# Head norms on ScalarE, and the gates of two channel tiles ahead of the key projection, in a streaming encoder layer

## The chip, the cores and the metric

The kernel runs on one NeuronCore of a Trainium2 chip. The metric is device time in microseconds (us) for one execution; lower is better. Engines: TensorE (PE; its weight loads are PEld), VectorE (DVE), ScalarE (ACT), GpSimd (POOL) and SyncE (SP), whose queue issues the transfers.

## The reference

One layer of a chunk-causal encoder, for a prompt of 1024 tokens and a sample batch of 8 x 16 tokens (1152 tokens, nine tiles of 128). What matters here is the first sub-layer:

```python
h = rmsnorm(x, g_mix)
z = h @ w_in                                   # 1024 -> 2560
zq, zk, zv, zu = jnp.split(z, [512, 1024, 1536], axis=-1)
q = rmsnorm(zq.reshape(B, T, 4, 2, 64), g_q)   # each head map of 64 on its own
k = rmsnorm(zk.reshape(B, T, 4, 2, 64), g_k)   # k is an output too
...                                            # differential attention on q, k, v
a, gate = jnp.split(zu, 2, axis=-1)
c = a * jax.nn.sigmoid(gate)                   # 512 channels
c_hist = jnp.concatenate([c_past, c], axis=1)
cv = jax.nn.silu(layernorm(depthwise_causal_conv(c_hist, w_conv, b_conv), ln_g, ln_b))   # 31 taps
x = x + jnp.concatenate([o, cv], axis=-1) @ w_out
```

A memory cross-attention and a squared-ReLU MLP follow. All is in float32. `rmsnorm` divides by the root of the mean square plus 1e-6.

## The kernel before

**Products.** Every large product is made of three matmuls, on operands that are split in a high and a low part (`mm3`, lines 123 to 125). The split of a weight unit (`load_w`) is a transfer into one of four raw buffers, a cast on ScalarE (line 113) and a subtraction on VectorE or GpSimd (line 116); it lands in a pool of eight units ("w") or, for some, in a second of two ("wx"). In the stages looked at here the subtraction is on VectorE.

**Projections.** The normalised and transposed input stays in on-chip memory. After channel tiles 0 and 1 of the gates come three projections, `wi` = 0, 1, 2 for Q, K and V, each with eight weight units and nine token tiles. `project(wi, wu, t)` makes 24 matmuls into one PSUM bank (of eight in the pool). For Q and K it then takes the norm of each of the eight 64-wide heads: ScalarE squares the whole 512 (line 374), VectorE reduces to eight sums (376), GpSimd adds epsilon (377) and raises to the power -1/2 (`rpow`, line 139), VectorE multiplies the bank with the eight values into `zn` (380). `zn` is stored (383, 385), and for K VectorE also makes the output `ko` with the gain (388). The tiles `sq` and `ko` share a tag with two buffers. For V ScalarE copies the bank (366).

**Convolution.** The 512 channels are four channel tiles `ct` of 128. For each, `start_conv` reserves the gate output `cp` (prompt) and `cs` (samples), two buffers each, has GpSimd clear the first 30 columns (344), and loads four weight units. `history` brings the past. `gated` multiplies, for three groups of three token tiles, the gate half and then the linear half, each into a bank; ScalarE takes a tanh of the first (290, one buffer) and VectorE writes the product into `cp` and `cs` (293, 296). `conv_taps` then runs 31 taps on VectorE, each one instruction of 1024 columns for the prompt (305 for the first, 307) and one of 128 for the samples (326, 328), and stores the accumulators (331, 332). The prompt's accumulator `acc` has one buffer. `conv_state` writes the last gate outputs out.

**Order.** The taps are a chain of generators, `taps`; one step of it is two taps, and 16 steps are a channel tile. Tile 0's first 768 columns are done while the gates of tiles 0 and 1 run. After each token tile of a projection `TP[wi]` steps are taken, with TP = (4, 2, 2). Channel tile 2 has its gates between Q and K, tile 3 between K and V. This is the order in which the program is written; the order of each engine's queue is drawn up from it by a scheduler that estimates when an instruction is ready, and is then fixed.

**Attention.** After the V projection the pools of the projections and of the convolution are given back, and their memory is taken by the attention stage: the prompt's scores and softmax (`attend`), the products with the values by way of the transposed weights `wT` (`values`, lines 699 to 704), the sample batch's attention over the cache, and `conv_norm`, which reads the stored accumulators. Reuse of memory waits for its last reader, the accumulators' store among them.

Of the kernel before, what the change touches and what calls it, by code (L numbers as in the profile page):

```python
# [12 lines left out]
AF = mybir.ActivationFunctionType  # L13
ALU = mybir.AluOpType
# [4 lines left out]
P = 128  # L19
# [17 lines left out]

WB, RB, VB, KB, UB = 8, 4, 3, 4, 2

TP, HP = (4, 2, 2), 2  # L40

EL = 3

# [21 lines left out]
def kernel(  # L65
# [187 lines left out]
    def history(ct, cs):  # L253
        hist = cv.tile([120, 2, P], F32, name=f"hist{ct}", tag="hist", bufs=1)
        for j in range(2):
            sp.dma_start(hist[:, j, :], cache_conv[0, 4 * j:4 * j + 4, :, ct * P:(ct + 1) * P].rearrange("b t c -> (b t) c"))
        ps = bank(f"hi{ct}")
        for j in range(2):
            pe.transpose(ps[:, j * 120:(j + 1) * 120], hist[:, j, :], ident[:120, :120])
        dve.tensor_scalar_mul(cs[:, :, 0:30], ps[:, :240].rearrange("p (b t) -> p b t", t=30), 2.0)  # L260
# [56 lines left out]
    def conv_taps(ct, cp, cs, lo=0):  # L317
        if lo == 0:
            accs[ct] = cv.tile([P, 1024], F32, name=f"acc{ct}", tag="acc", bufs=1)
        acs = cv.tile([P, P], F32, name=f"acs{ct}", tag="acs")  # L320
        av = acs.rearrange("p (b t) -> p b t", t=16)
        for j in range(31):
            prompt_tap(ct, cp, j, lo, 1024)
            wj = wc[:, ct, j:j + 1]
            if j == 0:
                dve.tensor_scalar(av, cs[:, :, 0:16], wj, col("b_conv", ct), op0=ALU.mult, op1=ALU.add)
            else:
                dve.scalar_tensor_tensor(out=av, in0=cs[:, :, j:j + 16], scalar=wj, in1=av, op0=ALU.mult, op1=ALU.add)
            if j % 2:
                yield  # L330
        sp.dma_start(dacc[ct, :, 0:1024], accs[ct])
        sp.dma_start(dacc[ct, :, 1024:1152], acs)
        yield
# [7 lines left out]
    def start_conv(ct):  # L341
        cp = cv.tile([P, 1054], F32, name=f"cp{ct}", tag="cp")
        cs = cv.tile([P, 8, 46], F32, name=f"cs{ct}", tag="cs")
        pool.memset(cp[:, 0:30], 0.0)
        raws = load_wz(ct)
        if ct:
            convs[ct] = (cp, cs, split_wz(ct, raws))
        else:
            convs[ct] = (cp, cs, raws)

    def run(it):
        for _ in it:
            pass
# [6 lines left out]
    def project(wi, wu, t):  # L360
        ps = bank(f"z{wi}_{t}")
        for k in range(KT):
            mm3(ps, tok(hT, k, t, 0), tok(hT, k, t, 1), wu[k][:, 0, :], wu[k][:, 1, :], k == 0, k == KT - 1)
        zn = wk.tile([P, 512], F32, name=f"zn{wi}_{t}", tag="zn", bufs=3)
        if wi == 2:
            act.copy(zn, ps)
            sp.dma_start(vf[t].rearrange("t h e -> t (h e)"), zn)
            if t < 8:
                sp.dma_start(dv[t * P:(t + 1) * P, :], zn)
            else:  # L370
                pool.tensor_copy(v8, zn)
            return
        sq = wk.tile([P, 512], F32, name=f"sq{wi}_{t}", tag="sq")
        act.activation(sq, ps, AF.Square, scale=0.125)
        ms = sm(8, "ms8")
        dve.tensor_reduce(out=ms, in_=sq.rearrange("p (a d) -> p a d", a=8), axis=AX.X, op=ALU.add)
        pool.tensor_scalar_add(ms, ms, EPS)
        rs = sm(8, "rs8")
        rpow(rs, ms, 8)
        dve.tensor_mul(zn.rearrange("p (a d) -> p a d", a=8), ps.rearrange("p (a d) -> p a d", a=8),  # L380
                       rs.unsqueeze(2).broadcast_to([P, 8, 64]))
        if t < 8:
            sp.dma_start(dq[wi][t * P:(t + 1) * P, :], zn)
        else:
            sp.dma_start(d8[wi], zn)
        if wi == 1:
            ko = wk.tile([P, 512], F32, name=f"ko{t}", tag="sq")
            dve.tensor_mul(ko.rearrange("p (a d) -> p a d", a=8), zn.rearrange("p (a d) -> p a d", a=8),
                            gkb.unsqueeze(1).broadcast_to([P, 8, 64]))
            sp.dma_start(kf[t].rearrange("t h c -> t (h c)"), ko)  # L390
# [139 lines left out]
    for wi in range(3):  # L530
        wu = load_qkv(wi)
        for t in range(NT):
            project(wi, wu, t)
            if t == 0:
                for ct in ((0, 1), (2,), (3,))[wi]:
                    conv_state(ct, *convs[ct][:2])
            run(islice(taps, TP[wi]))
            if wi == 2 and t == EL:
                load_half(1, 0, 0)
                load_half(0, 0, 0)  # L540
                for j in range(KB):
                    load_keys(0, j)
        if wi < 2:
            ct = wi + 2
            start_conv(ct)
            history(ct, convs[ct][1])
            for g in range(3):
                run(gated(ct, g, *convs[ct]))
            taps = chain(taps, conv_taps(ct, *convs[ct][:2]))
    run(taps)  # L550
    p1.close()
    pg.close()
# [1111 lines left out]
```

## Time and profile before

| | |
|---|---|
| timed runs | 1578.28, 1606.75, 1607.65 us (median 1606.75) |
| the profiled execution | 1578.97 us, its span 1577.2 us, mean granted TensorE clock 0.985 |
| TensorE busy | 1501.8 us (95% of the span), weight loads 1296.0 (82%) |
| VectorE busy | 1086.6 us (69%), 2020 instructions |
| ScalarE busy | 731.9 us (46%), 1530 instructions |
| GpSimd busy | 242.9 us (15%), 374 instructions |
| transfers | 237.88 MB, 151 GB/s over the span |

In the profiled execution the Q projection runs from 80 to 132 us, the gates of channel tile 2 to 157, K to 207.5, the gates of tile 3 to 233.7, and V to 284.5. A busy TensorE is not one at its peak, as matmuls overlap; idle time of an engine counts only where the end waits for it. Times in rows are us from the start of the span unless marked ns; what stands in square brackets at the end of a timeline row is the engine's idle time ahead of it and what ended it.

### The profile page before, as it was taken

Reading aid. Unit: us, or ns where it says so; the run is one execution under the profiler, and the core shown is the slowest. Engines: PE = TensorE matmul, PEld = TensorE weight load, DVE = VectorE, ACT = ScalarE, POOL = GpSimd, SP = SyncE. Lnnn points to the kernel's source line nnn. Section 1 sums busy time; section 2 is a strip of 40 time slices with the busy share of each in tenths; the row PEclk is TensorE's granted clock in tenths of the full one; section 3 lists DMA queues with packets and bytes.
Section 4 is the critical chain, followed back from the end, with each engine's and each line's share of the span. In section 5 each row is a group of like instructions: output and inputs, shape, how many; then the busy total and the mean of one; then the engine's idle time right before and its main releaser. Section 6 shows DMA issues by size and latency. Waiting matters only on the chain.

```text
span 1577.2 us, 25642 instructions
## 1 busy us (share of the span) xinstructions
PE 1501.8 (95%) x9326; PEld 1296.0 (82%) x9326; DVE 1086.6 (69%) x2020; ACT 731.9 (46%) x1530; POOL 242.9 (15%) x374
## 2 busy tenths in 40 slices
PE   6999999779898899999999899999999999999998
PEld 6989898457686787787678899999999888778887
DVE  5899899967566664534857786676566556996565
ACT  5312021478677742634656444444353444544442
POOL 3051530041544431131011000000000000000000
PEclk9999999899999999999999999999999999999999
DMA  6333242477775733112432554444574566743343
GB/s 201 129 95 107 85 142 110 157 253 251 237 227 160 252 108 104 47 47 88 138 104 95 156 196 154 154 149 130 167 231 136 170 206 215 241 130 109 119 141 94
DMA packets 187121, 237.88 MB, mean 151 GB/s; under 512 B 23851, under 2 KB 101717, under 8 KB 186996
## 3 DMA queue, kind: packets, MB, share of 16 engines
q1 hardware_dynamic: 186996, 236.25, 46.9%
q8 instruction: 73, 1.20, 0.3%
q14 instruction: 52, 0.43, 0.1%
HBM read 172.59 MB, written 63.60 MB: 150 GB/s over the span
## 4 chain that ended last, share of the span: by engine, by line
PE 78%; DVE 7%; DMA 5%; ACT 4%; POOL 2%; issue 2%; SPq 1%; DVEq 0%; ACTq 0%
PE p L124 13%; PE p L125 13%; PE p L123 13%; PE pj L123 3%; PE pj L125 3%; PE pj L124 3%; PE z L123 2%; PE z L124 2%; PE z L125 2%; PE zu L125 2%; PE zu L123 2%; DVE acc L307 2%; PE zu L124 2%; PE po L704 2%; PE kT L768 1%
## 5 line engine op out<-in xcount | busy, mean ns | idle before, releaser
L124 PE MATMUL p<-Bp,Ap 128*128 128x512 f32 x448 | 175.8, 392 | 1.4 <-DVE Bp L1532 1.4
L125 PE MATMUL p<-Bp,Ap 128*128 128x512 f32 x448 | 174.9, 391 | 0.0
L307 DVE SCALAR_TENSOR_TENSOR acc<-cp,wc,acc 128x1024 f32<-128x1024 f32 (+2 forms) x150 | 158.7, 1066 | 0.7
L123 PE MATMUL p<-Bp,Ap 128*128 128x512 f32 x448 | 158.1, 390 | 1.0 <-ACT Bp L1531 1.0
L1531 ACT CAST Ap<-w_xb 128x512 fp32r<-128x512 f32 x112 | 69.5, 621 | 160.6 <-PE p L125 138.8
L1532 DVE TENSOR_TENSOR Ap<-w_xb,Ap 128x512 fp32r<-128x512 f32 x112 | 77.3, 690 | 90.0 <-ACT Ap L1531 90.0
L123 PE MATMUL p<-b_t,s 128*128 128x288 f32 x384 | 114.4, 298 | 4.5 <-DVE o L1378 4.5
L124 PE MATMUL p<-b_t,s 128*128 128x288 f32 x384 | 114.3, 298 | 0.0
L125 PE MATMUL p<-b_t,s 128*128 128x288 f32 x384 | 113.9, 298 | 0.3 <-DVE s L1285 0.3
L124 PEld LDWEIGHTS p<-Bp,Ap 128*128 128x128 f32 x448 | 84.6, 189 | 21.4 <-DVE Bp L1532 3.8
L123 PEld LDWEIGHTS p<-Bp,Ap 128*128 128x128 f32 x448 | 84.1, 188 | 18.8 <-ACT Bp L1531 1.4
L125 PEld LDWEIGHTS p<-Bp,Ap 128*128 128x128 f32 x448 | 84.6, 189 | 17.5
L123 PE MATMUL z<-wqkv,h 128*128 128x512 f32 x216 | 86.0, 398 | 0.0
L125 PE MATMUL z<-wqkv,h 128*128 128x512 f32 x216 | 85.4, 395 | 0.0
L124 PE MATMUL z<-wqkv,h 128*128 128x512 f32 x216 | 85.3, 395 | 0.0
L123 PEld LDWEIGHTS p<-b_t,s 128*128 128x128 f32 x384 | 72.9, 190 | 4.7 <-ACT s L1284 4.7
L123 PE MATMUL p<-b_b,a 128*128 128x288 f32 x256 | 75.7, 296 | 0.0
L124 PE MATMUL p<-b_b,a 128*128 128x288 f32 x256 | 75.7, 296 | 0.0
L125 PE MATMUL p<-b_b,a 128*128 128x288 f32 x256 | 75.6, 296 | 0.0
L1368 ACT ACTIVATE o<-o 128x576 f32<-128x576 f32 x64 | 43.8, 685 | 68.4 <-DVE o L1378 28.2
L124 PEld LDWEIGHTS p<-b_t,s 128*128 128x128 f32 x384 | 73.1, 190 | 0.0
L125 PEld LDWEIGHTS p<-b_t,s 128*128 128x128 f32 x384 | 72.3, 189 | 0.6 <-DVE s L1285 0.6
(511 smaller groups left out, 4237.8 us busy)
## 6 DMA issues: line engine op xcount, KB each, us to landing
kr<-in_cache_k_dram SPq DMA_DIRECT2D x32, 512.0 KB
vu<-in_cache_v_dram SPq DMA_DIRECT2D x32, 512.0 KB
w1t<-in_w_ff_dram SPq DMA_DIRECT2D x32, 512.0 KB
w_xb<-ds SPq DMA_DIRECT2D x64, 256.0 KB
da<-o SPq DMA_DIRECT2D x48, 256.0 KB
w_xb<-da SPq DMA_DIRECT2D x48, 256.0 KB
ds<-o SPq DMA_DIRECT2D x32, 256.0 KB
dxr<-XP SPq DMA_DIRECT2D x18, 256.0 KB
```

What stands on the lines that cost most here:

```text
L123: pe.matmul(out, lh, rh, start=first, stop=False)
L124: pe.matmul(out, lh, rl, start=False, stop=False)
L125: pe.matmul(out, ll, rh, start=False, stop=last)
L307: dve.scalar_tensor_tensor(out=out, in0=cp[:, lo + j:hi + j], scalar=wj, in1=out, op0=ALU.mult, op1=ALU.add)
L704: pe.matmul(po, wT[:, j * P:(j + 1) * P], vss[h][jb][:, j], start=4 * jb + j == 0, stop=4 * jb + j == i)
L768: pe.transpose(ps[:, h * 256 + t * P:h * 256 + (t + 1) * P], kr[:, t, (2 * hp + h) * P:(2 * hp + h + 1) * P], ident)
L1368: act.activation(c, c, AF.Relu)
L1531: act.copy(u[:, 0], src)
L1532: dve.tensor_sub(u[:, 1], src, f32(u[:, 0]))
```

## The change

The reduction and the product of the norm go from VectorE to ScalarE. In place of one Square over 512 columns there are eight over 64, each with its sum taken by the instruction (`accum_out`), and in place of the product on VectorE eight copies, each scaled by its head's value. GpSimd's two steps stay. The gates of channel tiles 2 and 3 both come between Q and K, with three tap steps after each of their six groups (GP = 3); TP becomes (3, 2, 2). The convolution state of tile 3 is written in the K projection instead of the V projection.

```diff
--- before.py
+++ after.py
@@ -37,7 +37,7 @@
 
 WB, RB, VB, KB, UB = 8, 4, 3, 4, 2
 
-TP, HP = (4, 2, 2), 2
+TP, HP, GP = (3, 2, 2), 2, 3
 
 EL = 3
 
@@ -371,14 +371,15 @@
                 pool.tensor_copy(v8, zn)
             return
         sq = wk.tile([P, 512], F32, name=f"sq{wi}_{t}", tag="sq")
-        act.activation(sq, ps, AF.Square, scale=0.125)
         ms = sm(8, "ms8")
-        dve.tensor_reduce(out=ms, in_=sq.rearrange("p (a d) -> p a d", a=8), axis=AX.X, op=ALU.add)
+        heads = [slice(a * 64, a * 64 + 64) for a in range(8)]
+        for a, c in enumerate(heads):
+            act.activation(sq[:, c], ps[:, c], AF.Square, scale=0.125, accum_out=ms[:, a:a + 1])
         pool.tensor_scalar_add(ms, ms, EPS)
         rs = sm(8, "rs8")
         rpow(rs, ms, 8)
-        dve.tensor_mul(zn.rearrange("p (a d) -> p a d", a=8), ps.rearrange("p (a d) -> p a d", a=8),
-                       rs.unsqueeze(2).broadcast_to([P, 8, 64]))
+        for a, c in enumerate(heads):
+            act.activation(zn[:, c], ps[:, c], AF.Copy, scale=rs[:, a:a + 1])
         if t < 8:
             sp.dma_start(dq[wi][t * P:(t + 1) * P, :], zn)
         else:
@@ -532,7 +533,7 @@
         for t in range(NT):
             project(wi, wu, t)
             if t == 0:
-                for ct in ((0, 1), (2,), (3,))[wi]:
+                for ct in ((0, 1), (2, 3), ())[wi]:
                     conv_state(ct, *convs[ct][:2])
             run(islice(taps, TP[wi]))
             if wi == 2 and t == EL:
@@ -540,13 +541,14 @@
                 load_half(0, 0, 0)
                 for j in range(KB):
                     load_keys(0, j)
-        if wi < 2:
-            ct = wi + 2
-            start_conv(ct)
-            history(ct, convs[ct][1])
-            for g in range(3):
-                run(gated(ct, g, *convs[ct]))
-            taps = chain(taps, conv_taps(ct, *convs[ct][:2]))
+        if wi == 0:
+            for ct in (2, 3):
+                start_conv(ct)
+                history(ct, convs[ct][1])
+                for g in range(3):
+                    run(gated(ct, g, *convs[ct]))
+                    run(islice(taps, GP))
+                taps = chain(taps, conv_taps(ct, *convs[ct][:2]))
     run(taps)
     p1.close()
     pg.close()
```

## Rows read from the trace of the kernel before

**Rows 1.** the chain of waits that ended last: each engine's share of the span

```profile
PE 78%; DVE 7%; DMA 5%; ACT 4%; POOL 2%; issue 2%; SPq 1%; DVEq 0%; ACTq 0%
```

**Rows 2.** stretch, length; busy PE, PEld, DVE, ACT, POOL; clock, DMA share, GB/s

```profile
157.00:207.50 50.50, 50.50 (x220) 40.54 (x219) 42.72 (x63) 7.42 (x14) 25.53 (x14) 1.00 0.25 84
...
233.70:284.50 50.80, 50.76 (x220) 40.43 (x218) 47.43 (x62) 5.24 (x10) 2.47 (x3) 1.00 0.31 112
285.00:300.00 15.00, 9.30 (x66) 6.39 (x66) 13.27 (x21) 9.36 (x20) 1.69 (x3) 0.89 0.78 246
300.00:312.00 12.00, 8.73 (x45) 5.19 (x42) 11.56 (x22) 4.15 (x10) 0.97 (x1) 0.59 0.28 100
312.00:333.00 21.00, 13.99 (x154) 8.84 (x153) 13.85 (x26) 11.58 (x28) 8.71 (x11) 0.91 0.57 186
333.00:345.00 12.00, 10.08 (x80) 6.73 (x79) 7.14 (x21) 11.37 (x27) 3.35 (x7) 1.00 1.07 340
...
365.00:400.00 35.00, 32.02 (x364) 26.19 (x364) 24.26 (x72) 27.16 (x71) 7.37 (x16) 1.00 0.86 268
```

**Rows 3.** VectorE's last taps: its groups after 284.5, timeline, and the chain at 327

```profile
L307 DVE SCALAR_TENSOR_TENSOR acc<-cp,wc,acc 128x1024 f32<-128x1024 f32 x22 | 28.1, 1280 | 0.1
...
325.84 1.28 DVE L307 SCALAR_TENSOR_TENSOR acc<-cp,wc,acc 128x1024 f32<-128x1024 f32 x1
...
332.26 0.29 DVE L701 COPY wT<-pT 128x128 f32<-128x128 f32 x1 [4.48 <-DMA dacc<-acc]
...
327.15 5.03 DMA dacc<-acc
```

**Rows 4.** VectorE's groups of 80 to 284.5 us: busy, mean ns, idle before

```profile
L380 DVE TENSOR_TENSOR zn<-z,rs 128x512 f32<-128x512 f32 x18 | 12.4, 687 | 9.0 <-POOL rs L139 8.9
L376 DVE TENSOR_REDUCE ms<-sq 128x8 f32<-128x512 f32 x18 | 12.2, 681 | 1.8 <-ACT sq L374 1.7
```

**Rows 5.** timeline of GpSimd and VectorE where a buffer is waited for

```profile
138.04 0.12 POOL L344 MEMSET cp<- 128x30 f32 x1 [1.41 <-DVE acc L307]
...
272.50 0.81 DVE L305 TENSOR_SCALAR acc<-cp,wc,cols 128x1024 f32<-128x1024 f32 x1 [3.05 <-DMA dacc<-acc]
```

**Rows 6.** ScalarE's timeline in the attention, and its Square in the projections (ns)

```profile
334.81 0.37 ACT L715 ACTIVATE o<-po,f 128x128 f32<-128x128 f32 x1 [0.34 <-POOL f L139]
335.08 1.25 ACT L800 ACTIVATE sp<-sp,smn 128x1152 f32<-128x1152 f32 x1
...
338.80 0.28 ACT L708 ACTIVATE o<-po 128x128 f32<-128x128 f32 x1
338.97 0.19 ACT L708 ACTIVATION_READ_ACCUMULATOR o<-po 128x1 f32 x1
339.06 0.61 ACT L113 CAST wmk<-wmk_1r 128x512 fp32r<-128x512 f32 x1
...
L374 ACT ACTIVATE sq<-z x18: 574/598/602, 86.5 to 220.6; 128x512 f32<-128x512 f32 x18
```

**Rows 7.** GpSimd's two steps of a norm, Q tile then K tile

```profile
95.42 0.26 POOL L377 TENSOR_SCALAR ms<-ms 128x8 f32<-128x8 f32 x1
95.76 1.67 POOL L139 TENSOR_TENSOR rs<-ms,neghalf 128x8 f32<-128x8 f32 x1
...
171.75 1.20 POOL L377 TENSOR_SCALAR ms<-ms 128x8 f32<-128x8 f32 x1 [3.47 <-DVE ms L376]
173.03 2.80 POOL L139 TENSOR_TENSOR rs<-ms,neghalf 128x8 f32<-128x8 f32 x1
```

**Rows 8.** ScalarE and TensorE at the junction of the K projection and the gates

```profile
212.85 0.62 ACT L113 CAST wqkv<-wqkv_2r 128x512 fp32r<-128x512 f32 x1 [6.71 <-DMA wqkv_2r<-in_w_in_dram]
...
212.75 0.45 PE L125 MATMUL zu<-h,wz 128*128 128x384 f32 x1 [0.63 <-DVE wz L116]
```

## The prediction, made before the changed kernel ran

> **What bounds the kernel now.** I read the chain of waits first. TensorE carries 78% of it, VectorE 7% [rows 1], so a step counts only where TensorE waits, and the next view is the table by stage [rows 2]. The K projection (157 to 207.5 us) is TensorE without a gap: 50.50 busy of 50.50 us, 50.5/9 = 5.61 us a token tile. The V projection (233.7 to 284.5) is the same, 50.76 of 50.80. So in the stages that the change edits there is nothing for TensorE to win. Just behind them there is: from 285 to 333 us it is busy 9.30 + 8.73 + 13.99 = 32.0 us of 48, while VectorE is full (13.27 of 15, 11.56 of 12) until 312. The granted clock is 0.89, 0.59 and 0.91 of full there: from 300 to 312 mostly the lower level of 1.2 GHz, after 15 us in which TensorE worked 9.30.
>
> What VectorE does there is convolution taps of the last channel tile. Between 284.5 and 340 us it still runs 22 of them, 28.1 us in all; the last starts at 325.84, the store of the accumulator lands 5.03 us after 327.15, and only then, at 332.26, does VectorE make the first transposed weight tile wT, having waited 4.48 us for that landing [rows 3]. The wT tiles take over the memory of the convolution pool, so no product with the values runs before. The late taps cost twice: they share VectorE with the scores of the first attention tiles, and they lock the second half of attention.
>
> **What is removed.** Per tile of Q and K, VectorE loses the reduction and the product with the inverse norm: 18 x (0.681 + 0.687) = 24.6 us busy, of which about 0.08 us each overlapped the next instruction, so 18 x 1.2 = 21.8 us of queue. It also loses the idle time ahead of that product, 9.0 us waiting for GpSimd's power [rows 4]. Together 30.8 us less in the queue that ends with the last tap.
>
> **What the moved gates do.** Before, channel tile 3 could not start before its gates at 207.5 to 233.7; but its first tap started at 272.50, after 3.05 us for the store of tile 2's accumulator (the accumulator has one buffer) [rows 5]. The taps run one channel tile after another, and the gates of 3 were not what they waited for. So the move alone I cost at nothing for the start of the taps; what it gives is the room in program order to use the 30.8 us. Tap steps allotted before were 36, 18 and 18 over the three projections for 16 a channel tile, so tile 3's last came in the eighth V tile; now 27 + 18 + 18 + 18 are allotted, and 64 are used up in the first V tile.
>
> The move has its own wait. There are two buffers of gate output, so channel tile 3's gates write where tile 1's taps still read. GpSimd's clearing of the buffer shows this wait for tile 2 (138.04, 1.41 us for the last tap of tile 0) [rows 5]. After the change tile 0 ends near 127 (138.0 less 9 x 1.2), and tile 1 some 60 us later, near 187: 31 taps of 1.28 us with their sample shares are about 45, and 16 weight subtractions and the gate products the rest. TensorE computes tile 3's gates at 157 to 183. Behind the clearing on GpSimd stand the copies of the convolution state and the norms of the first K tiles; on VectorE the gate products; on ScalarE, with one buffer for the tanh, the second and third tanh. Five of eight PSUM banks are held by then, three K tiles (17 us) fit in the rest: cost nothing, or up to 5 us if the banks run out. Also moved ahead of the K weights are eight small weight loads, two history loads on SP's queue, four ScalarE casts and four VectorE subtractions; the 25 us of the first gates hide them, as they hid four of each before.
>
> **Where the taps end.** 327 - 30.8 = 296; and of the 48 us behind 285 some 16 us of VectorE are attention work that the earlier taps no longer share. So the last tap comes near 285, between 281 and 296, and wT is free near 290 instead of 332.
>
> **What that is worth (A).** The 32.0 us of TensorE work at the rate of 365 to 400 us (32.02 of 35, or 0.915) [rows 2] would take 35.0: a gain of 13.0. What is late next are the transfers: 15 x 0.78 + 12 x 0.28 + 21 x 0.57 + 12 x 1.07 = 39.9 us of full DMA stand in the 60 us from 285 to 345, which at the 0.86 share of 365 to 400 take 46, a gain of at most 14. If TensorE never waited it would be 48 - 32.0 = 16; if loads and short chains hold the entry anyway, 0. I take 11, near the 13, less 2 for the first loads, whose wait remains.
>
> **What ScalarE gets.** No row has 64 columns. The nearest are the same instructions at 128: a Square with a sum starts at 338.80, its accumulator is read at 338.97, and the next instruction starts at 339.06, so 0.26 us a pair; a copy scaled by a column starts at 334.81, the next instruction at 335.08, so 0.27 [rows 6]. Between 128 and 512 columns the Square grows by (0.598 - 0.28)/384 = 0.83 ns a column, so 64 fewer save 0.05: 0.21 and 0.22. Eight of each: 1.7 + 1.7 = 3.4 us in place of 0.6 a tile. If nothing overlapped it would be 0.23 + 0.19 and 0.32 each, 5.9 a tile. That is 18 x 2.8 = 50 us (or 95) more of ScalarE in stages where it is busy 7.42 of 50.5; off TensorE's path so long as it keeps up with 5.61 us a tile.
>
> The wait for GpSimd now stands in ScalarE's queue. Behind it are the next tile's Squares, the tanh of the gates and the casts of the next weights; TensorE waits for the last. GpSimd's two steps take 0.26 + 1.67 = 1.9 us in the Q projection at best, but 1.20 + 2.80 = 4.0 in the K projection, where they stand beside 1.28 us taps [rows 7]. Squares, GpSimd, copies are 1.7 + 4.0 + 1.7 = 7.4 us a tile if the copies stand straight behind the Squares, against 5.61: 1.8 behind a tile, 16 at the ninth. In the trace GpSimd always starts just as a tap does, since the reduction stands ahead of the tap; after the change the instant is arbitrary, so half of the 2.1 us of delay is the likelier: 6.4 a tile, 7 us behind at the end.
>
> The Trainium skill, in "SBUF — State Buffer" (SBUF: two separate sides), says that VectorE and GpSimd share a port pair as an exclusive lock: a VectorE instruction with two SBUF inputs blocks a GpSimd one that reads SBUF for its whole length. By that rule each of the two steps can lose at most one tap, 4.5 us in all; the trace agrees with 4.0. By it ScalarE would be 16 us behind, were the taps still in step; by arbitrary instants 7.
>
> **The junction of K and V (B).** Before, gates stood between each two projections and hid the loading of eight weight units. Now the V weights follow the K weights directly, with ten slots for converted units and four raw ones. Two V units can be ready early; unit k needs the slot that the last K tile frees at its step k-2, which is 5.6 + 0.7 = 6.3 us ahead of need. If ScalarE is 7 us behind, the first late unit costs 1 us; the last two raw loads can only start when two units are converted, and such a load has kept ScalarE idle for 6.71 us, while TensorE lost 0.63 at that junction to a late subtraction [rows 8]. I take 4 us: 1 for the lag, 3 for the raw loads. Ends: 0 if the casts come in time, as at the start of the K and V projections [rows 2], and 16 - 6.3 + 4 = 14 if ScalarE is 16 behind.
>
> **Sum.** The profiled execution took 1578.97 us, its span 1577.2 and 1.8 around it. 1579 - 11 + 4 = 1572. The three timed runs are 1578.28, 1606.75 and 1607.65, median 1606.75; the profile belongs to the lowest, and I forecast in its terms. Why the others are 1.8% longer no row shows; at that level the same forecast is 1572 x 1607.65/1578.97 = 1600.6.
>
> **Rivals.**
> - *The entry is held by transfers.* The taps end early and TensorE still waits for keys, values and their conversion: for it, the DMA share of 1.07 at 333 to 345 [rows 2]; against it, the share of 0.28 at 300 to 312 in the middle of the gap, and the named wait for the accumulator. A is 2: 1581.
> - *The taps do not end earlier.* Buffers of gates or accumulator, or the order in which the queues are written, leave the last tap near 327. For it: the three waits of this kind (1.41, 3.05 and 4.48 us); against: none is near the 30.8 us that fall away. 1579 to 1583.
> - *ScalarE becomes the chain.* Place: the first V tile, waiting for casts behind the scaled copies. Price: with instructions half way between the 3.4 and the 5.9 us a tile, 4.6 + 4.0 = 8.6 us, 27 behind at the ninth tile, less 6.3, plus 4: 25 us. 1579 + 25 - 11 = 1593. It decides from about 13 us of lag, where B eats A. Without any overlap (9.9 a tile) it gives 1604. For it: the 4.0 us of GpSimd (six of the nine K tiles have the durations of the row shown); against: the starts 0.26 and 0.27 us apart [rows 6], and eight banks, which let ScalarE fall three to four tiles behind before TensorE stops inside a projection.
>
> The Trainium skill speaks for this rival: "ScalarE: Activation LUTs" (Rules for kernel authors) puts multiplications on VectorE, not ScalarE. The trace agrees on engine time, 2.8 us added for 1.2 saved a tile; it says nothing on whose queue is late.
>
> **How the numbers follow.** Forecast 0.55 (its own range 1563 to 1582), entry held 0.15, taps not earlier 0.09, ScalarE the chain 0.17, a larger gain than 16 through the clock of 0.59 in the gap 0.04. All but the ends lie within 2% of 1579 (1547 to 1610), about what a measurement of this kernel can tell from no change. Beyond: faster 0.08, slower 0.08, each mostly the two levels of the runs, 1.8% apart, meeting an error of a few us. Range: from 1579 - 16, with some 6 us more for the clock, 1557, to the forecast at the upper level and the worst of ScalarE, 1603.
>
> **What would show it.** Right: the last tap between 281 and 296 and the first wT within 8 us of it; TensorE busy over 38 of the 48 us that follow the V projection; eight Squares and eight copies about 0.2 us apart; TensorE gap-free in Q and K, with a gap under 6 us at the first V tile. Wrong: a tap beyond 310; ScalarE's copies running more than 13 us behind the tile's last matmul; DMA share near 1 with TensorE idle after 285. The forecast fails most easily in the order of the queues, which is drawn up for the new program anew and may differ far from the edit.

## The result and the profile after

The changed kernel takes 1590.23 us (median of 12 runs, 1586.53 to 1592.33); the kernel before took 1571.10 to 1578.91 beside it, with disturbed runs (those near 1600 us) left out, as they are in all ratios, with one of 2951 us of experiment E10. The ratio is 1.0094, 95% interval [1.0082, 1.0105]: slower by 0.9%, where 1572 us, 0.4% less than the profiled 1578.97, was forecast. The profiled execution took 1590.97 us, its span is 1589.2, 12.0 more than before.

I read the chain of waits first, as before; the page gives its shares by engine and then by line.

```profile
PE 68%; DVE 10%; ACT 7%; POOL 6%; DMA 5%; issue 2%; SPq 1%; DVEq 0%; ACTq 0%; POOLq 0%
PE p L124 12%; PE p L125 12%; PE p L123 12%; POOL rs L139 4%; PE pj L123 3%; PE pj L125 3%; PE pj L124 3%; DVE acc L307 2%; PE zu L123 2%; PE zu L124 2%; PE zu L125 2%; ACT zn L382 2%; ACT sq L377 2%; PE po L706 1%; PE q L123 1%
```

TensorE fell from 78% [rows 1] to 68%, and GpSimd rose from 2 to 6%, of which 4% is one line, the power of the norms. Where it stands in time is in GpSimd's timeline (start, length):

```profile
89.06 1.38 POOL L512 MEMSET biasm<- 128x1536 f32 x1
90.41 30.58 POOL L139 TENSOR_TENSOR rs<-ms,neghalf 128x8 f32<-128x8 f32 x1
123.48 0.25 POOL L378 TENSOR_SCALAR ms<-ms 128x8 f32<-128x8 f32 x1 [2.49 <-ACT sq L377]
123.81 1.66 POOL L139 TENSOR_TENSOR rs<-ms,neghalf 128x8 f32<-128x8 f32 x1
```

The first power, on 128x8 values, lasted 30.58 us; the next one, of the same size, 1.66. Before, it took 1.67 to 2.80 [rows 7]. VectorE's timeline over the same time shows what else ran (a row can hold several alike, counted at its end):

```profile
90.08 1.40 DVE L307 SCALAR_TENSOR_TENSOR acc<-cp,wc,acc 128x768 f32<-128x768 f32 x2
91.41 0.60 DVE L328 SCALAR_TENSOR_TENSOR acs<-cs,wc,acs 128x128 f32<-128x128 f32 x2
...
118.56 0.89 DVE L328 SCALAR_TENSOR_TENSOR acs<-cs,wc,acs 128x128 f32<-128x128 f32 x3
...
119.49 0.35 DVE L328 SCALAR_TENSOR_TENSOR acs<-cs,wc,acs 128x128 f32<-128x128 f32 x1
...
119.87 0.35 DVE L328 SCALAR_TENSOR_TENSOR acs<-cs,wc,acs 128x128 f32<-128x128 f32 x1
146.06 0.81 DVE L305 TENSOR_SCALAR acc<-cp,wc,cols 128x1024 f32<-128x1024 f32 x1 [25.83 <-DMA dacc<-acc]
```

Taps of the prompt and taps of the samples follow one another, each starting before the last has ended (90.08 + 1.40 = 91.48, the next starts at 91.41; the overlap is 0.07 to 0.10 us). 81 of them start while the power is open. The first gap is one of 0.04 us, ahead of the last tap but one (118.56 + 0.89 = 119.45, the next starts at 119.49), and 1.54 us after it, at 120.99, the power ends: about the length that it has alone.

The overlap alone doesn't explain it. The same run of overlapping taps, without a gap, was there before the power started, and GpSimd's addition of epsilon for the same tile got in:

```profile
86.93 0.57 POOL L378 TENSOR_SCALAR ms<-ms 128x8 f32<-128x8 f32 x1 [0.89 <-ACT convp L272]
86.38 1.40 DVE L307 SCALAR_TENSOR_TENSOR acc<-cp,wc,acc 128x768 f32<-128x768 f32 x2
```

It ended at 87.50, 0.12 us after the first of these two taps (86.38 to 87.38), though the second had started by then. Of the ten steps of the norms that start in the projections while a two-input instruction of VectorE is overlapped by another, eight get in like this, at once or at the end of the instruction that is running; two are held on to the end of the run of taps, this power and an addition of 3.81 us at 228.06.

After the power, VectorE in its turn stands for 25.83 us, until the accumulator is stored. What waits in between is in the waits of three engines; here ScalarE's and then TensorE's (total, times, longest):

```profile
ACT zn L382 <- POOL rs L139: 40.0, 7, 28.2
```

```profile
PE zu L123 <- ACT wz L113: 21.6, 1, 21.6
PE st L265 <- DVE cp L293: 4.5, 1, 4.5
PE z L123 <- ACT wqkv L113: 1.7, 2, 0.9
PE zu L123 <- ACT zn L382: 1.6, 1, 1.6
```

ScalarE's scaled copies wait 28.2 us for the power. SyncE's queue waits for those copies (57.7 us in eight waits, the longest 30.1), as the stores of the normed tiles stand in it ahead of the accumulator's store, which is issued at 143.15 although the taps ended at 120.2. ScalarE then works off the Q tiles at 5.3 us each, and the casts of the gate weights stand behind; TensorE waits 21.6 us for one of them. In the table by stage (columns as in rows 2) the loss stands as a stretch of 26.6 us with 3.40 busy, and a K projection of 58.2 where 50.5 stood before [rows 2]:

```profile
79.00:130.40 51.40, 51.40 (x227) 41.32 (x225) 40.91 (x105) 9.77 (x71) 38.95 (x14) 1.00 0.17 50
130.40:157.00 26.60, 3.40 (x17) 2.90 (x16) 5.55 (x6) 18.16 (x122) 9.77 (x11) 0.64 0.20 75
157.00:207.10 50.10, 50.10 (x278) 50.06 (x277) 48.89 (x79) 13.96 (x49) 4.21 (x5) 0.95 0.26 79
207.10:265.30 58.20, 53.68 (x224) 42.82 (x223) 49.18 (x69) 24.78 (x167) 23.00 (x17) 0.94 0.27 96
265.20:318.20 53.00, 51.20 (x219) 40.29 (x218) 46.25 (x42) 16.12 (x70) 6.76 (x6) 1.00 0.41 144
318.20:330.00 11.80, 7.82 (x47) 6.21 (x46) 9.57 (x22) 9.10 (x20) 2.19 (x4) 0.71 0.87 286
```

The sum closes: the V projection ends at 318.2, before at 284.5, so 33.7 us are lost up to there. From its end to the first matmul of the memory cross-attention (`tg_cross`) it was 640.5 - 284.5 = 356.0 us before and is 651.5 - 318.2 = 333.3: 22.7 come back. From there to the end 1.0 is lost. 33.7 - 22.7 + 1.0 = 12.0, the difference of the spans.

### The profile page after: what moved, and what is told of

The parts are those of the page before. It is cut to its first block, busy times and chain, and to the rows that moved or that the text cites. A ratio compares the mean times of both kernels' runs of the same rounds, so it can differ in the third digit from the quotient of the medians.

```text
span 1589.2 us, 26029 instructions
## 1 busy us (share of the span) xinstructions
PE 1498.3 (94%) x9326; PEld 1297.0 (82%) x9326; DVE 1070.0 (67%) x1984; ACT 781.1 (49%) x1944; POOL 255.7 (16%) x374
## 4 chain that ended last, share of the span: by engine, by line
PE 68%; DVE 10%; ACT 7%; POOL 6%; DMA 5%; issue 2%; SPq 1%; DVEq 0%; ACTq 0%; POOLq 0%
PE p L124 12%; PE p L125 12%; PE p L123 12%; POOL rs L139 4%; PE pj L123 3%; PE pj L125 3%; PE pj L124 3%; DVE acc L307 2%; PE zu L123 2%; PE zu L124 2%; PE zu L125 2%; ACT zn L382 2%; ACT sq L377 2%; PE po L706 1%; PE q L123 1%
## 5 line engine op out<-in xcount | busy, mean ns | idle before, releaser
L123 PE MATMUL zu<-h,wz 128*128 128x384 f32 x192 | 65.9, 349 | 27.0 <-ACT wz L113 21.6
L139 POOL TENSOR_TENSOR rs<-ms,neghalf 128x1 f32<-128x1 f32 (+2 forms) x46 | 86.3, 1876 | 3.8
L1370 ACT ACTIVATE o<-o 128x576 f32<-128x576 f32 x64 | 43.8, 685 | 68.7 <-DVE o L1380 28.1
L123 PEld LDWEIGHTS p<-b_t,s 128*128 128x128 f32 x384 | 73.2, 191 | 5.0 <-ACT s L1286 5.0
```

What stands on the lines that cost most here:

```text
L123: pe.matmul(out, lh, rh, start=first, stop=False)
L139: pool.tensor_tensor(out, ms, neghalf[:, :n], op=ALU.pow)
L1370: act.activation(c, c, AF.Relu)
```

## The experiments

The first theory: GpSimd's power is shut out of memory as long as VectorE's tap instructions, which read two tensors, overlap one another; VectorE's own wait for that power was what ended such a run of taps before, and the change took the wait away. A second loss, the 4.5 us of `st` for `cp`, comes from the moved gates. The rivals are in the expectations. All kernels are timed against the kernel before, in five rounds, but E5 (one profiled run). A step of GpSimd is called held when it doesn't get in by the end of the tap that is running, nor of the next.

**E1. Norms alone**, gates where they were: the kernel before with only this part of the change.

```diff
-        act.activation(sq, ps, AF.Square, scale=0.125)
-        dve.tensor_reduce(out=ms, ...)
+        for a, c in enumerate(heads):
+            act.activation(sq[:, c], ps[:, c], AF.Square, scale=0.125, accum_out=ms[:, a:a + 1])
...
-        dve.tensor_mul(zn..., ps..., rs...)
+        for a, c in enumerate(heads):
+            act.activation(zn[:, c], ps[:, c], AF.Copy, scale=rs[:, a:a + 1])
```

> Head norms on ScalarE as in the changed kernel, gates and tap steps as in the kernel before. Theory A (GpSimd is shut out while VectorE runs taps that overlap one another): the first Q tile's power takes over 15 us again, ScalarE's queue stands behind it, TensorE loses 15 to 25 us where the gates of channel tile 2 begin; 1585 to 1605 us. Rival B (the sixteen small ScalarE instructions a tile are the cost): power under 5 us, ScalarE steadily behind, 1580 to 1600. Rival C (the move of the gates is the cost): as before or faster, 1560 to 1578.

1584.42 us, ratio 1.0062 [1.004, 1.0083]. The first power took 30.58 us again, and TensorE waited in the same place:

```profile
PE zu L123 <- ACT wz L113: 21.9, 2, 21.6
PE zu L123 <- ACT zn L382: 1.6, 1, 1.6
```

The first loss belongs to the norms alone; the time is just under the expected 1585.

**E2. Gates alone**, norms on VectorE: the changed kernel with E1's edit turned back.

```diff
-TP, HP = (4, 2, 2), 2
+TP, HP, GP = (3, 2, 2), 2, 3
...
+        if wi == 0:
+            for ct in (2, 3):
+                start_conv(ct)
+                ...
```

> Gates of channel tiles 2 and 3 moved as in the changed kernel, the norms on VectorE as before. Theory A: GpSimd's power stays under 4 us since VectorE waits for it, no gap in TensorE over 5 us between 80 and 285 us; 1570 to 1585 us. Rival B: the same. Rival C: slower than before, 1585 to 1600, with TensorE idle where the V projection follows the K projection.

1583.13 us, ratio 1.0059 [1.004, 1.0079]. No power is over 2.80 us, and TensorE has one wait in the projections:

```profile
PE st L265 <- DVE cp L293: 15.7, 1, 15.7
```

In this part alone the second loss is 15.7 us, which no expectation had: theory A allowed no gap over 5 us, and rival C had it behind the K projection. Its path: GpSimd clears `cp` of channel tile 3 at 199.66, after 8.43 us for a tap of tile 1; the gate products on VectorE follow, to 202.06 + 0.42; and the transposes of tile 3's cached rows, which the change put behind the first K tile, stand in TensorE's queue ahead of the second.

**E3. The change with a wait given back.** After each power VectorE copies its eight values to an unused tile, and so has to wait for it.

```diff
+        seen = sm(8, "seen8")
+        dve.tensor_copy(seen, rs)
```

> The changed kernel, plus one VectorE copy of the eight inverse norms of each Q and K tile into an unused tile, so that VectorE waits for GpSimd as it did before. Work is only added. Theory A: the power takes under 4 us in every tile, the TensorE gap of some 23 us ahead of the gates is gone, and it is faster than the changed kernel by 15 to 30 us: 1560 to 1575 us. Rival B: ScalarE does the same sixteen instructions a tile, so it stays at 1585 to 1595. Rival C: the same as B.

1571.75 us, ratio 0.9984 [0.9969, 0.9999], from 1.0094. Eighteen copies were added and the kernel is 1.1% faster. Six steps are still held, for 1.35 to 2.88 us, and each gets in where VectorE stops for its copy. The longest power is 2.88 us, and of the 21.6 us 2.5 are left; the wait for `cp` stays, with 5.5:

```profile
PE st L265 <- DVE cp L293: 5.5, 1, 5.5
PE zu L123 <- ACT wz L113: 2.5, 1, 2.5
```

**E4. The change with all taps in one order.** The taps of the prompt come first and those of the samples behind, each issued after the one before, so that each reads what the last one wrote and none overlap; no waits for GpSimd.

```diff
+    def chained(make):
+        with tc.issue_after(behind[-1]) if behind else ExitStack():
+            behind.append(make().ins)
...
-            dve.scalar_tensor_tensor(out=out, in0=cp[:, lo + j:hi + j], ...)
+            chained(lambda: dve.scalar_tensor_tensor(out=out, in0=cp[:, lo + j:hi + j], ...))
```

> The changed kernel with all taps in one fixed order on VectorE (the prompt's 31, then the samples' 31 of a channel tile), so that each tap waits for the one before and none overlaps the next. Same instructions, two SBUF inputs each. Theory A: a gap of some 35 ns between taps lets GpSimd in after at most one tap, power under 5 us in every tile, no gap of TensorE ahead of the gates; taps are slower by 0.1 us each, some 25 us of VectorE in all; 1565 to 1582 us. If any two-input instruction shuts GpSimd out, overlapped or not, the first power stays over 15 us and the time at 1590 or above.

1577.58 us, ratio 1.0022 [1.0005, 1.0038]. One run of 30 dependent taps in VectorE's timeline, and GpSimd's 18 powers over the projections (busy, mean ns, idle before):

```profile
95.31 15.60 DVE L312 SCALAR_TENSOR_TENSOR acc<-cp,wc,acc 128x256 f32<-128x256 f32 x30
```

```profile
L139 POOL TENSOR_TENSOR rs<-ms,neghalf 128x8 f32<-128x8 f32 x18 | 38.9, 2163 | 1.5
```

Each of these taps takes 0.485 us, and 15.60/30 = 0.520 from one to the next: 0.035 us of gap. VectorE has the same two-input taps as in the changed kernel, and never waits for GpSimd, yet no power took over 2.67 us (mean 2.16; in the changed kernel 3.61). In the projections TensorE waits 1.0 us for a cast and 2.0 at their head for a transfer, and V ends at 284.1. So two-input taps as such, without overlap, hold no step. The time is nevertheless that of the kernel before: the prompt's last tap comes at 316.1, but the samples' last, which now stands behind it, at 336.8, and `wT` at 338.9.

**E5. Overlapping taps with one input.** Each tap after the first, of the prompt (shown) and of the samples, is written as the first is; this leaves out the convolution's sum over the taps.

```diff
-            dve.scalar_tensor_tensor(out=out, in0=cp[:, lo + j:hi + j], scalar=wj, in1=out, op0=ALU.mult, op1=ALU.add)
+            dve.tensor_scalar(out, cp[:, lo + j:hi + j], wj, col("b_conv", ct), op0=ALU.mult, op1=ALU.add)
```

> The changed kernel with every tap after the first written as a one-input instruction, without adding to the accumulator: the convolution's sum over taps is left out. Theory (two-input instructions that overlap shut GpSimd out): taps with one input let GpSimd in, so no power over 3 us in the projections. Rival (any instructions of VectorE that follow each other without a gap shut GpSimd out, one input or two): the first power takes over 10 us, as long as taps are there to issue. Its time says little, since the taps are shorter or longer; it is looked at for the power and for TensorE's waits between 120 and 160 us.

VectorE's rows and GpSimd's, at the place where the changed kernel was shut out:

```profile
95.44 0.41 DVE L307 TENSOR_SCALAR acc<-cp,wc,cols 128x256 f32<-128x256 f32 x1
95.77 0.60 DVE L328 TENSOR_SCALAR acs<-cs,wc,cols 128x128 f32<-128x128 f32 x2
96.28 0.41 DVE L307 TENSOR_SCALAR acc<-cp,wc,cols 128x256 f32<-128x256 f32 x1
```

```profile
93.22 1.84 POOL L139 TENSOR_TENSOR rs<-ms,neghalf 128x8 f32<-128x8 f32 x1
...
98.01 1.72 POOL L139 TENSOR_TENSOR rs<-ms,neghalf 128x8 f32<-128x8 f32 x1
```

The taps overlap as before (95.44 + 0.41 = 95.85, the next starts at 95.77), and the powers pass among them, the longest at 2.74 us; TensorE waits nowhere between 80 and 170 us. One-input taps delay GpSimd too, but by a tap at a time: among taps of 0.81 us four powers in turn take 2.41. So a long hold was seen only with both, two inputs and overlap. That it needs two inputs rests on this one execution, in which thirteen steps start under overlapping one-input instructions.

**E6. One wait only**, in the first Q tile.

```diff
+        if wi == 0 and t == 0:
+            seen = sm(8, "seen8")
+            dve.tensor_copy(seen, rs)
```

> The changed kernel with the waiting VectorE copy in the first Q tile alone. Theory A (overlapping taps shut GpSimd out, whichever tile): the first power takes under 4 us and that of one of the next Q tiles over 10; 1575 to 1592 us. If there is something special about the first power (a first use in the stage), all are under 5 us and the time is at or below that of the run with waits in every tile, 1565 to 1574.

1582.15 us, ratio 1.005 [1.003, 1.007]. The first power is 2.88 us, and two tiles later the adding of epsilon is shut out instead:

```profile
102.78 19.94 POOL L378 TENSOR_SCALAR ms<-ms 128x8 f32<-128x8 f32 x1 [2.89 <-ACT sq L377]
122.81 1.72 POOL L139 TENSOR_TENSOR rs<-ms,neghalf 128x8 f32<-128x8 f32 x1
```

VectorE's rows at its end:

```profile
122.03 0.60 DVE L328 SCALAR_TENSOR_TENSOR acs<-cs,wc,acs 128x128 f32<-128x128 f32 x2
...
122.66 0.35 DVE L328 SCALAR_TENSOR_TENSOR acs<-cs,wc,acs 128x128 f32<-128x128 f32 x1
```

The taps overlap up to 122.03 + 0.60 = 122.63, the next comes 0.03 us later, and 0.10 us after the start of that gap, at 102.78 + 19.94 = 122.72, the addition is over. So it isn't something about the power: the addition can be held as well, and a gap of 0.03 us is enough to let it in. But not every step that meets overlapping taps is held. One tile earlier the same addition started at the same point of the same tap:

```profile
97.23 0.86 POOL L378 TENSOR_SCALAR ms<-ms 128x8 f32<-128x8 f32 x1 [2.49 <-ACT sq L377]
96.97 1.41 DVE L307 SCALAR_TENSOR_TENSOR acc<-cp,wc,acc 128x768 f32<-128x768 f32 x2
102.52 1.41 DVE L307 SCALAR_TENSOR_TENSOR acc<-cp,wc,acc 128x768 f32<-128x768 f32 x2
```

Both started 0.26 us after the start of a tap of 768 columns that the next one overlapped; one took 0.86 us, the other 19.94. What decides between them no run shows. TensorE's wait for the cast is 15.2 us here.

**E7, E8, E9. Tile 3's cached rows back in the V projection**: in the change (E7), in E2 (E8) and in E3 (E9).

```diff
-                for ct in ((0, 1), (2, 3), ())[wi]:
+                for ct in ((0, 1), (2,), (3,))[wi]:
```

E7: 

> The changed kernel with one edit: the cached rows of channel tile 3 are prepared in the value projection again, not in the key projection. Theory (two separate losses in the changed kernel): only the 4.5 us wait of the key projection's transposes for the copy on VectorE goes; GpSimd's first power still takes about 30.6 us and TensorE still waits about 21.6 us for the gate weights' casts, so the projections end near 313 us and the time is 1583 to 1588 us. Rival 1 (the two losses are one: what is late in the queue of VectorE is late for the transposes too, and the first loss covers the second): no change, 1589 to 1592 us. Rival 2 (moving the rows relieves GpSimd as well): first power under 10 us and a time under 1575 us.

E8: 

> Gates moved alone, norms on VectorE, and the convolution state of tile 3 in the V projection. If the state's transposes are the whole price of the move: the gap of 15.7 us is gone, 1565 to 1574 us. If the late taps hold TensorE in another way (banks held by tile 3's gates): the gap moves, 1576 to 1586.

E9: 

> The run in which VectorE waits for the inverse norms, with one more edit: the convolution state of channel tile 3 is written in the V projection again (its transposes no longer stand in TensorE's queue behind the first K tile). If those transposes, which need tile 3's gates, which need tile 1's taps, are what stops TensorE in the K projection: the gap of 5.5 us ahead of them is gone, K takes 51 to 54 us in place of 59.7, 1560 to 1569 us. If the banks or the casts stop it as well, the gap only moves to another instruction and the time stays at 1569 to 1576.

The wait for `cp` is gone in all three. E8 takes 1578.25 us, 1.0032 [1.0017, 1.0047], where E2 had 1.0059; E9 1568.37, 0.9967 [0.9952, 0.9982], where E3 had 0.9984. E8 missed its expectation: the gap went and moved nowhere, V ends at 284.7 as before, and still the time lies in the range given for a gap that moves; the last tap comes at 326.9, the first `wT` at 337.8. But E7 takes 1589.41, 1.0094 [1.0065, 1.0124], just the ratio of the change. My expectation of 1583 to 1588 missed, and the rival's figure held, though not for its reason: TensorE's waits are as the theory had them,

```profile
PE zu L123 <- ACT wz L113: 21.6, 1, 21.6
```

and V ends 7.6 us earlier, at 310.6, but the last tap starts at 326.3 in place of 320.8 and the first `wT` comes at 330.4 (329.7 in the change). With taps that late the end of V doesn't set the start of the attention's second half.

**E10. E1 with E3's waits**: norms on ScalarE, gates where they were, VectorE waiting.

```diff
         rpow(rs, ms, 8)
+        seen = sm(8, "seen8")
+        dve.tensor_copy(seen, rs)
```

> Norms on ScalarE with the gates at their old places, plus the VectorE copy that waits for the inverse norms. With GpSimd let in, ScalarE's sixteen instructions cost nothing: no TensorE gap over 5 us from 80 to 285 us, last tap between 295 and 312 (326 before), 1562 to 1573 us. If ScalarE's instructions cost time by themselves: 1576 or more, with TensorE waiting for ScalarE in the gates or the projections.

1564.74 us, ratio 0.9939 [0.992, 0.9958]: the fastest of all, ahead of both kernels. No power is over 2.88 us, and the last tap starts at 303.94. The V projection, the stretch up to the first `wT`, and that to `tg_cross`:

```profile
241.00:291.80 50.80, 50.80 (x222) 40.84 (x220) 49.32 (x60) 5.24 (x10) 2.46 (x3) 1.00 0.29 103
291.80:310.00 18.20, 13.45 (x78) 9.67 (x77) 14.71 (x30) 11.28 (x25) 2.77 (x5) 0.72 0.80 256
310.00:627.50 317.50, 291.28 (x2491) 238.24 (x2491) 202.53 (x506) 209.29 (x499) 112.89 (x183) 0.98 0.62 202
```

**E11. E1 with E4's order of taps.** The edit is E4's, in E1.

```diff
-            dve.scalar_tensor_tensor(out=out, in0=cp[:, lo + j:hi + j], ...)
+            chained(lambda: dve.scalar_tensor_tensor(out=out, in0=cp[:, lo + j:hi + j], ...))
```

> Norms on ScalarE, gates at their old places, and all taps in one order in which each depends on the one before, so that no two of them overlap; no waiting copies on VectorE. Theory (GpSimd is shut out only while VectorE's two-input instructions overlap): no power over 3 us in the projections, no wait of TensorE over 3 us there, projections end by 286 us, time 1564 to 1576 us depending on when the last tap comes. Rival (with the gates at their old places it is VectorE's waits for the gates that let GpSimd in or not, whatever the taps do): a power over 10 us stays and the time is 1580 us or more.

1578.30 us, ratio 1.0014 [0.9996, 1.0031]: no change, a little over the expected range. In the projections TensorE waits only 2.1 us, at their head for a transfer, and V ends at 284.5; but one power takes 3.74 us, over the 3 expected (it starts under a tap that two overlapping subtractions of VectorE follow), and the last tap of the prompt comes at 315.2, that of the samples at 334.0.

Side by side (us; "GpSimd" is the longest single step of the norms; "last tap" is the prompt's; the last column is from the end of V to `tg_cross`):

| kernel | ratio | GpSimd | V ends | last tap | first wT | V to tg_cross |
|---|---|---|---|---|---|---|
| before | 1 | 3.20 | 284.5 | 325.8 | 332.3 | 356.0 |
| the change | 1.0094 | 30.58 | 318.2 | 320.8 | 329.7 | 333.3 |
| E1 norms alone | 1.0062 | 30.58 | 309.9 | 318.8 | 327.1 | 339.6 |
| E2 gates alone | 1.0059 | 3.21 | 301.0 | 316.9 | 324.7 | 345.7 |
| E3 change, waits | 0.9984 | 2.88 | 300.3 | 303.5 | 312.4 | 337.7 |
| E4 change, taps in line | 1.0022 | 2.67 | 284.1 | 316.1 | 338.9 | 357.1 |
| E6 change, one wait | 1.005 | 19.94 | 311.2 | 313.7 | 322.7 | 334.1 |
| E7 change, rows in V | 1.0094 | 30.59 | 310.6 | 326.3 | 330.4 | 347.2 |
| E8 gates alone, rows in V | 1.0032 | 3.21 | 284.7 | 326.9 | 337.8 | 356.7 |
| E9 change, waits, rows in V | 0.9967 | 2.87 | 288.5 | 304.7 | 309.9 | 344.9 |
| E10 norms alone, waits | 0.9939 | 2.88 | 291.8 | 303.9 | 308.9 | 335.7 |
| E11 norms alone, taps in line | 1.0014 | 3.74 | 284.5 | 315.2 | 336.9 | 358.8 |

The parts can be priced from it, by ratios on 1575 us (1590.23/1.0094). GpSimd shut out: the change to E3, 0.0110 or 17.3 us (net of what the added copies cost). The cached rows in the K projection: E3 to E9, 0.0017 or 2.7 us. What is left of moving the gates: E10 to E9, 0.0028 or 4.4 us. The norms on ScalarE with GpSimd let in: E10, 0.0061 or 9.6 us of gain. -9.6 + 4.4 + 2.7 + 17.3 = 14.8 us, 0.0094 of 1575: it is one path of single edits from E10 to the change, and on another the prices differ (E7). By the intervals of the ratios the 2.7 us aren't clear of noise, and the 4.4 only just.

## Why the prediction was wrong

**The failed step** is the price of GpSimd's delay: "each of the two steps can lose at most one tap, 4.5 us in all", and "half of the 2.1 us of delay is the likelier". The rows of before that I read it from (2.80 for 1.67) show steps that got in at the end of a tap, and so did most others there: of 31 that start in the projections under overlapping two-input instructions, 30 got in by the end of the tap that was running. I took a usual loss for the largest one. One step was held before too, in the first Q tile, as in the changed kernel (there the power, here the addition ahead of it):

```profile
90.36 3.20 POOL L377 TENSOR_SCALAR ms<-ms 128x8 f32<-128x8 f32 x1
92.04 1.41 DVE L307 SCALAR_TENSOR_TENSOR acc<-cp,wc,acc 128x768 f32<-128x768 f32 x2
93.57 0.69 DVE L376 TENSOR_REDUCE ms<-sq 128x8 f32<-128x512 f32 x1
```

It stood for six taps and ended at 93.56, 0.11 us after VectorE paused (92.04 + 1.41 = 93.45) ahead of its next reduction. VectorE's own steps of the norm, with their pauses, the 1.8 us for the Squares and the 9.0 us for the powers [rows 4], kept such a hold short. I booked the 9.0 us as a gain of the change. Without these pauses the price of a held step isn't one tap but what is left of the run of taps, 30.58 us. The place was right: the text named the wait for GpSimd in ScalarE's queue, the casts behind it, and TensorE behind the casts; E1 shows that this part of the change alone makes the loss, E3 that a wait of VectorE undoes it, and E4, E11 and E5 that without overlap, or with one input, no step was held for long. Which of the steps that meet overlapping two-input taps are held stays open.

The Trainium skill, in "SBUF — State Buffer" (SBUF: two separate sides), says that whichever of the two engines starts first gets the pair of ports for a whole instruction, that the other fully blocks, and that deep queues would have to be drained to share. I took from it a loss of one instruction. The trace agrees for most steps (in the changed kernel eight of ten got in by the end of the instruction that was running), and E5 goes with its condition, two inputs in SBUF, so far as long holds go. The 30.58 us, during which 81 instructions started, show that the end of the running instruction isn't the limit of the loss: a step that isn't let in there can stand until VectorE leaves a gap. That it is these ports is the page's account; the runs show when GpSimd stands and when it doesn't.

**Where the taps end.** 285 was forecast (281 to 296) and 320.8 came. The 25.83 us in which VectorE stood for the accumulator's store account for most of the 36; they are the same loss by way of SyncE's queue, in which the store stood behind the Q tiles' stores. I had counted the accumulator's single buffer (3.05 us [rows 5]) and not what could come ahead of its store. With GpSimd let in the last tap comes at 303.9 (E10), where VectorE waits 14.0 us in the added copies, 18.9 behind the forecast. Of the two terms of the forecast, the 16 us of attention work were too many: by rows 2 and 3 VectorE is busy for 13.27 + 11.56 + 13.85 = 38.7 us from 285 to 333, of which 28.1 are taps, so 10.6 are left.

**The moved gates**, "cost nothing, or up to 5 us if the banks run out". The banks never ran out. What I walked past is an instruction that the diff moves in plain sight: the preparation of tile 3's cached rows. I named the clearing's wait for tile 1's taps and put the end of these near 187 us; in E2 the clearing runs at 199.66, and the transposes stand in TensorE's own queue, ahead of the second K tile. 15.7 us there, 4.5 in the change, 5.5 in E3. The wait's price depends on what is late already: taking it out lowers the ratio by 0.0027 after E2, by 0.0017 after E3 (not clear of noise) and not measurably in the change (E7). The count of tap steps was off as well: while tile 2's gates run only five of the nine steps asked for are left, so the 64th falls in the third V tile, not the first; no run shows that it cost anything.

**Term A, the attention's entry**: 11 us forecast, 16 held for the most possible. It was 22.7 in the change and 356.0 - 335.7 = 20.3 in E10, where V ends less late (291.8). The mechanism was right, the size too small. The same stretch of the kernel before, in two parts:

```profile
284.50:333.00 48.50, 32.02 (x259) 20.42 (x260) 39.18 (x67) 25.55 (x58) 11.36 (x15) 0.82 0.56 181
333.00:640.50 307.50, 281.07 (x2310) 229.57 (x2309) 194.48 (x486) 198.28 (x467) 109.37 (x173) 0.98 0.62 195
```

TensorE is busy for 32.02 + 281.07 = 313.1 of 356.0 us; in E10 for 13.45 + 291.28 = 304.7 of 335.7. The idle time went from 42.9 to 31.0, 11.9 less, which is the 11 I had. The other 8.4 us are busy time of as many matmuls (2567 in both). The granted clock accounts for part of it: the lower level, 1.2 GHz, is granted for 30.7 of the 356.0 us before and for 20.5 of the 335.7 in E10, and 10.2 us at half the clock are worth 5. What the other 3 are isn't shown. I had seen the clock of 0.59 [rows 2] and gave a larger gain through it a chance of 0.04, when it belonged in the sum.

**Term B, the junction of K and V**: 4 us forecast, 1.7 measured (TensorE's waits for the casts of `wqkv`, two, the longest 0.9). Right in kind, under the estimate.

**ScalarE's instructions**: 3.4 us a tile was forecast. In the changed kernel the eight copies take 1.75 us,

```profile
121.02 1.75 ACT L382 ACTIVATE zn<-z,rs 128x64 f32<-128x64 f32 x8 [28.20 <-POOL rs L139]
122.61 0.27 ACT L377 ACTIVATE sq<-z 128x64 f32<-128x64 f32 x1
122.72 0.26 ACT L377 ACTIVATION_READ_ACCUMULATOR sq<-z 128x1 f32 x1
122.81 0.28 ACT L377 ACTIVATE sq<-z 128x64 f32<-128x64 f32 x1
```

and a Square with its sum starts every 0.20 us (122.61, 122.81): 1.7 + 1.6. This held.

**The rivals.** "ScalarE becomes the chain" came nearest to the time (1593 against 1590.97), but by another cause than its price: the instructions were cheap and the lag was GpSimd's; and it stood at the gates behind Q, not at the first V tile. "The taps do not end earlier" named the outcome (320.8 against 325.8) and gave 1579 to 1583. "The entry is held by transfers" fell: with a DMA share of 0.80 to 0.87 behind V the entry still gained 20 us and more.

**Open.** Why E9, with the gates moved and both losses gone, is still 0.3% slower than E10: V ends 3.3 us earlier there, and the attention to `tg_cross` takes 344.9 in place of 335.7. Nor is a version without long holds and without VectorE's added copies fast: E4 and E11 end the prompt's taps at 315 to 316 and the samples' at 336.8 and 334.0, and the first `wT` follows 2 to 3 us later; what the order of the taps costs and what the 0.035 us per tap wasn't separated. And what lets one GpSimd step in between overlapping taps and holds the next (0.86 and 19.94 us in E6).

## What to carry to other kernels

Before a wait is counted as a saving, look at who uses it: here 9.0 us in which VectorE waited were also what kept a held GpSimd step short (3.20 us at most before, 30.58 after), and without them 17 us were lost. When VectorE gets a long run of independent two-input instructions, reckon with a GpSimd step held for the whole of it, though most aren't; look for every such step that falls into it and for what stands behind that step, through each in-order queue (ScalarE's casts, SyncE's stores) to the engine that sets the time. And where an edit moves a loop, follow each instruction in the loop to its own queue, not only those that the edit is about.

## What the runs showed of the hardware that was not expected

- A GpSimd instruction of 1.67 us took 30.58 us while VectorE ran two-input instructions that overlapped by 0.07 to 0.10 us, and ended 1.54 us after the first gap of 0.04 us between two of them; another of 0.23 to 0.25 us was held for 19.94 us and ended 0.10 us after such a gap. With a gap of 0.035 us ahead of each tap the longest power was 2.67 us; with one input and the same overlap 2.74. Under the same overlapping two-input instructions other steps got in at the end of the one that was running: eight of ten in the changed kernel, 30 of 31 in the kernel before.
- A kernel got faster by 1.1% through 18 added instructions of VectorE whose results nobody reads (E3).
- The same 21.6 us wait of TensorE came back to the tenth of a microsecond in three different programs (the change, E1, E7): the held power, which lasts as long as the run of taps up to its first gap, took 30.58, 30.58 and 30.59 us in them.
